# A two-layer hybrid decoder: the feed-forward layers in three parts of 6, 8 and 8 column pairs instead of four of 6, 6, 6 and 4, with a second Strassen double in the middle part, the gate's columns ahead of the up columns, and transfers queued behind those of the down projection

## The chip, the cores and the metric

One Trainium2 chip; the program runs on one of its cores. The time is the device time of one execution in microseconds, from the first to the last instruction and what lies around it; lower is better. PE is the matmul engine (PEld its weight loads), DVE the vector engine, ACT the activation engine, POOL the general engine, SP the engine that only issues transfers. [...] Each engine works through its own instructions in the order in which they were built, and waits where an operand isn't ready.

## The reference

The model has two layers on a stream of 512 tokens by 1024 features, all in float32. Layer 0 mixes with a state-space block, layer 1 with attention. Both end in the same feed-forward layer, which is all that the change touches:

```
def causal_dwconv(u, w, b):
    k_w = w.shape[0]
    s = u.shape[1]
    up = jnp.pad(u, ((0, 0), (k_w - 1, 0), (0, 0)))
    y = up[:, 0:s] * w[0]
    for k in range(1, k_w):
        y = y + up[:, k:k + s] * w[k]
    return y + b

def conv_ffn(x, ln_g, up_w, conv_w, conv_b, down_w):
    u = causal_dwconv(rms_norm(x, ln_g) @ up_w, conv_w, conv_b)
    gate, up = u[..., :FFN_DIM], u[..., FFN_DIM:]
    return (jax.nn.silu(gate) * up) @ down_w
```

`up_w` is 1024 x 5632 (2816 gate columns, then 2816 up columns), `conv_w` has three taps, `down_w` is 2816 x 1024. The result is added to the stream: `x = x + ff`.

## The kernel before, in words

**Precision and weights.** Every float32 matmul is made of three: each operand is split into a high half (an ACT copy to a rounded type) and a low half (a DVE subtraction), and high by high, high by low and low by high are added up in a PSUM bank (`mm3`, line 242). Weights stream from memory in chunks of 128 x 1024 into a ring of three raw tiles (`wr`), and are split into two rings of three tiles (`wh`, `wl`). The list `plan` holds all chunks in order; `chunk` (line 234) hands one to PE and has the split issued for two chunks ahead. When a chunk is issued, a function from `hooks` filed under its name is called: this is how a later step's loads are started.

**Pairs.** 128 gate columns and the 128 up columns of the same number make a pair; there are 22 (numbers 0 to 21). `whole` (line 1034) multiplies one pair by the normalised stream: two chunks of weights, each with half of the eight row blocks for both sides, 24 matmuls of 512 columns per chunk, gate and up taking turns. `taps` (line 1048) makes the convolution: one ACT instruction and two DVE instructions for each side; SiLU on ACT, the product on DVE (`gated`). `operands` (line 1291) then makes the seven token-side operands of a Strassen product for each two neighbouring pairs, a *double*: sums and high and low halves, in tiles `sh`, `sl`.

**Strassen doubles.** `double` (line 1149) computes two neighbouring pairs in another way: seven products (in the order 5, 1, 2, 6, 7, 3, 4) of 24 matmuls of 256 columns. Four of its weight combinations are made by transfers: a tile is loaded, and POOL's queue adds a second block to it (`up_plus`, line 1114), and a third once the first product's split has read it. `up_ahead` (line 1119) starts this: two loads on SP's queue, one accumulation on POOL's.

**Parts.** The 22 pairs are cut into parts (`PARTS_D`, line 32). When the pairs of a part are done, its down projection follows, again by seven Strassen products in the order of `SEVEN`: in layer 0 (`down_features`) of 256-column matmuls and features by tokens, in layer 1 (`down_tokens`) of 512 columns, added into `xr`. Weights come by loads (`down_load`) and accumulations (`plus`, line 1223): in layer 1 one tile `wz` serves products 1, 5, 6 and 4, each after one more accumulation. A part of four pairs in layer 1 has a form of its own (`short`), which adds with DVE instead.

**Order.** PE's order is written out: `KINDS` says for each part which doubles are plain (P) or Strassen (S); `STEPS` gives the steps of each part but the first, where P is a chunk of a plain pair, a digit a product of the Strassen double, and D the down projection of the part *before*. So each down projection starts two chunks (one pair) into the next part. The other engines' orders are made by the scheduler from the order of the program. Before, the second part of each layer had one Strassen double (pairs 8 and 9), and everything else was plain.

Of the kernel before, what the change touches and what calls it, by code (L numbers as in the profile page):

```python
# [18 lines left out]
P = 128  # L19
# [12 lines left out]
PARTS_D = (0, 6), (6, 12), (12, 18), (18, 22)  # L32
KINDS = "PPP", "PSP", "PPP", "PP"
STEPS = "PPPPPPPPPPPP", "PPDPPP51P26P734P", "PPDPPPPPPPPPP", "PPDPPPPPP"
# [10 lines left out]
def trunk_kernel(ctx: ExitStack, tc, x, ssm_ln_g, ssm_in_w, ssm_conv_w, ssm_conv_b, ssm_dt_bias,  # L45
# [84 lines left out]

# [898 lines left out]
    def ffn(l, norm, bp, gnext, nnext):  # L1029
        with (tc.tile_pool(name="ffn_h%d" % l, bufs=1) as hp, tc.tile_pool(name="ffn%d" % l, bufs=1) as fp,  # L1030
# [192 lines left out]
            def plus(t, p0, c, nq, j, i):  # L1223
                pool.dma_start(view(t, nq), source(p0, c, nq, j, i), accum_op=ALU.add)  # L1224

            def down_load(p0, n, k, c):
# [4 lines left out]
                sync.dma_start(view(raws[k][c], nq), source(p0, at, nq, j, i))  # L1231
                if k == "z" and not l:
                    plus(raws[k][c], p0, at, nq, 1, 1)
                if l and n == 4 and k != "y":
                    t, j = raws[k][1], k == "x"
                    sync.dma_start(view(t, nq), source(p0, at, nq, int(j), 0))
                    if not j:
                        plus(t, p0, at, nq, 0, 1)

            def short(m, p0, c, nq):  # L1240

                (z, z2), (x_, w), (y, _) = (raws[k] for k in "zxy")
                t = {"1": z, "2": w, "7": x_, "3": y}.get(m, z2)
                more = {"7": y, "6": y, "4": w}.get(m)
                if more is not None:
                    dve.tensor_tensor(out=t, in0=t, in1=more, op=ALU.add)
                return t

            def down_ahead(p0, n, ks):
                for k in ks:  # L1250
                    for c in range((n // 2 + 1) // 2 if l else 2):
                        down_load(p0, n, k, c)

            def combine(key, m, p0, c, nq):
# [5 lines left out]
                few = l and (p0, p0 + 4) in PARTS_D  # L1260
                if few:
                    t = short(m, p0, c, nq)
                elif m == "2" or (m == "4" and not l):
# [15 lines left out]
                if more and not few:  # L1279
# [269 lines left out]
            for i in range(1, len(parts)):  # L1549
# [7 lines left out]
                elif l:  # L1557
                    hooks[key] = lambda p0=p0, n=n: down_ahead(p0, n, "zxy")
# [483 lines left out]
```

## Time and profile before

| | us |
|---|---|
| three runs | 1350.83, 1354.39, 1353.06 (median 1353.06) |
| the profiled execution | 1350.98 |
| its span | 1349.3 |
| mean granted clock of the matmul engine | 0.991 of full speed |

The page's second part cuts the span into 40 equal slices of 33.7 us and gives the busy share of each in tenths:

```profile
PE   9999999999999999999997999999999989999997
PEld 8878888888887999988986778777888869788885
DVE  7899888788879867967759867678789857986877
PEclk9999999999999999999998999999999989999999
```

The feed-forward layer of layer 0 takes roughly slices 11 to 21, that of layer 1 slices 29 to 39; in between lies the attention. Times given as A:B are microseconds from the start of the span. In a list of waits a row names who waited at which line for whom, then the total, the number and the longest. A row of the chain has a start, a length, the engine, the tile and the line. The low halves of weights are `wl_h` (plain pairs), `wl_U` (Strassen doubles) and `wl_s` (down projection).

### The profile page before, as it was taken

How to read it: one execution, taken by the hardware profiler on the slowest of the kernel's cores; microseconds unless marked ns; L12 is line 12 of the kernel's file. 1: busy time of each engine (PE TensorE's matmuls, PEld its weight loads, DVE VectorE, ACT ScalarE, POOL GpSimd, SP SyncE). 2: the span in 40 equal slices, each digit the busy share in tenths (PEclk: the TensorE clock that was granted, in tenths of full speed). 3: DMA queues.
4: the chain of work that ended last, by engine and by line, in shares of the span. 5: the costliest groups of instructions: out<-in, count | busy, mean ns of one | idle time of the engine just before them, and what ended most of it. 6: DMA issues, size and time to landing. Idle time of an engine off the chain costs nothing.

```text
span 1349.3 us, 18914 instructions
## 1 busy us (share of the span) xinstructions
PE 1316.9 (98%) x6915; PEld 1106.9 (82%) x6915; DVE 1089.8 (81%) x1825; ACT 737.5 (55%) x1224; POOL 172.8 (13%) x205
## 2 busy tenths in 40 slices
PE   9999999999999999999997999999999989999997
PEld 8878888888887999988986778777888869788885
DVE  7899888788879867967759867678789857986877
ACT  6695554652567445544435657777566425544442
POOL 5320301200111310200203200000200110100100
PEclk9999999999999999999998999999999989999999
DMA  7543533431566893763743844221233664562631
GB/s 205 160 149 94 148 101 111 138 97 55 154 192 189 180 209 121 147 161 79 154 97 86 222 96 127 63 79 55 66 99 118 156 148 125 118 164 86 149 94 62
DMA packets 203005, 170.52 MB, mean 126 GB/s; under 512 B 9308, under 2 KB 176608, under 8 KB 202912
## 3 DMA queue, kind: packets, MB, share of 16 engines
q1 hardware_dynamic: 173728, 125.46, 31.1%
q0 software_dynamic: 25728, 38.56, 15.4%
q10 hardware_dynamic: 3456, 5.30, 1.2%
q8 instruction: 54, 0.88, 0.3%
q14 instruction: 39, 0.32, 0.1%
HBM read 162.84 MB, written 6.44 MB: 125 GB/s over the span
## 4 chain that ended last, share of the span: by engine, by line
PE 86%; DVE 7%; ACT 2%; DMA 2%; issue 1%; POOL 0%; DVEq 0%; SPq 0%; ACTq 0%; POOLq 0%
PE ps_in L243 5%; PE ps_in L245 5%; PE ps_in L244 5%; PE ps_g L245 5%; PE ps_g L243 5%; PE ps_g L244 5%; PE ps_u L243 5%; PE ps_u L244 5%; PE ps_u L245 5%; PE ps_s L1434 3%; PE ps_s L1429 3%; PE ps_s L1432 3%; PE ps_o L244 2%; PE ps_o L245 2%; PE ps_o L243 2%; PE ps_s L1333 2%
## 5 line engine op out<-in xcount | busy, mean ns | idle before, releaser
L245 PE MATMUL ps_g<-xgh,wl_h 128*128 128x512 f32 x320 | 124.6, 389 | 0.9 <-DVE wl_h L193 0.9
L243 PE MATMUL ps_g<-xgh,wh_h 128*128 128x512 f32 x320 | 124.9, 390 | 0.0
L244 PE MATMUL ps_g<-xgl,wh_h 128*128 128x512 f32 x320 | 124.6, 389 | 0.0
L243 PE MATMUL ps_u<-xgh,wh_h 128*128 128x512 f32 x320 | 124.6, 389 | 0.0
L244 PE MATMUL ps_u<-xgl,wh_h 128*128 128x512 f32 x320 | 124.5, 389 | 0.0
L245 PE MATMUL ps_u<-xgh,wl_h 128*128 128x512 f32 x320 | 124.5, 389 | 0.0
L243 PE MATMUL ps_in<-xgh,wh_in 128*128 128x512 f32 x304 | 122.9, 404 | 0.0
L245 PE MATMUL ps_in<-xgh,wl_in 128*128 128x512 f32 x304 | 119.7, 394 | 0.0
L244 PE MATMUL ps_in<-xgl,wh_in 128*128 128x512 f32 x304 | 119.2, 392 | 0.0
L182 ACT ACTIVATE wh_h<-wr_h 128x1024 fp32r<-128x1024 f32 x80 | 84.4, 1055 | 59.9 <-PE ps_u L244 33.9
L193 DVE TENSOR_TENSOR wl_h<-wr_h,wh_h 128x1024 fp32r<-128x1024 f32 x80 | 98.0, 1229 | 19.3 <-ACT wh_h L182 14.6
L1224 POOL DMA_DIRECT2D wz<-in_ffn_down_w_dram x43 | 51.3, 1258 | 468.7 <-DVE wl_s L1275 219.6
L1059 DVE SCALAR_TENSOR_TENSOR vg<-ps_g,cf,vg 128x511 f32<-128x511 f32 x72 | 53.8, 748 | 52.5 <-ACT vg L1057 51.9
L1074 ACT ACTIVATE sh<-vg 128x512 fp32r<-128x512 f32 (+1 forms) x88 | 48.9, 572 | 79.0 <-DVE vg L1146 52.7
L1432 PE MATMUL ps_s<-sh,wh_s 128*128 128x256 f32 x308 | 79.8, 286 | 6.7 <-ACT sh L1074 5.4
L1434 PE MATMUL ps_s<-sl,wh_s 128*128 128x256 f32 x308 | 79.8, 286 | 0.4 <-DVE sl L1075 0.2
L1274 ACT ACTIVATE wh_s<-wz 128x768 fp32r<-128x768 f32 (+2 forms) x52 | 43.4, 835 | 63.6 <-DMA wz<-in_ffn_down_w_dram 32.6
L1331 PE MATMUL ps_s<-wh_s,sh 128*128 128x512 f32 x153 | 61.9, 405 | 11.9 <-ACT wh_s L1274 6.5
L245 PEld LDWEIGHTS ps_g<-xgh,wl_h 128*128 128x128 f32 x320 | 60.1, 188 | 13.8 <-DVE wl_h L193 1.3
L245 PEld LDWEIGHTS ps_u<-xgh,wl_h 128*128 128x128 f32 x320 | 60.1, 188 | 12.6
L244 PEld LDWEIGHTS ps_u<-xgl,wh_h 128*128 128x128 f32 x320 | 60.1, 188 | 12.5
L243 PEld LDWEIGHTS ps_u<-xgh,wh_h 128*128 128x128 f32 x320 | 60.0, 188 | 12.5
(492 smaller groups left out, 3580.2 us busy)
## 6 DMA issues: line engine op xcount, KB each, us to landing
wr_h<-in_ffn_up_w_dram SPq DMA_DIRECT2D x160, 256.0 KB, 3.6
wr_in<-in_ssm_in_w_dram SPq DMA_DIRECT2D x40, 512.0 KB, 3.9
m<-cumd POOLq DMA_DIRECT2D x16, 512.0 KB, 4.3
wr_out<-in_ssm_out_w_dram SPq DMA_DIRECT2D x16, 512.0 KB, 3.5
wz<-in_ffn_down_w_dram POOLq DMA_DIRECT2D x18, 384.0 KB, 6.3
wz<-in_ffn_down_w_dram POOLq DMA_DIRECT2D x10, 512.0 KB, 5.8
wr_s<-in_ffn_down_w_dram SPq DMA_DIRECT2D x12, 384.0 KB, 3.4
xT<-in_ffn_down_w_dram SPq DMA_DIRECT2D x9, 512.0 KB, 5.5
```

The costliest lines, as they stand in the source:

```text
L182: return act.activation(self.wh[:, :self.n], self.raw[:, :self.n], AF.Copy)
L193: return eng.tensor_tensor(out=self.wl[:, :self.n], in0=self.raw[:, :self.n], in1=self.wh[:, :self.n].bitcast(F32), op=ALU.subtract)
L243: pe.matmul(ps, wh, xh, start=start, stop=False)
L244: pe.matmul(ps, wh, xl, start=False, stop=False)
L245: return pe.matmul(ps, wl, xh, start=False, stop=stop).ins
L1059: dve.scalar_tensor_tensor(out=v[:, s:], in0=u[:, :T - s], scalar=tap_col(j, p, 2 - s), in1=v[:, s:], op0=ALU.mult, op1=ALU.add)
L1074: act.activation(hi, v, AF.Copy)
L1224: pool.dma_start(view(t, nq), source(p0, c, nq, j, i), accum_op=ALU.add)
L1274: act.activation(wh[:, :n], t[:, :n], AF.Copy)
L1331: pe.matmul(pss[b], h, ws[q][0][:, cols], start=first and q == qs[0], stop=False, skip_group_check=more)
L1432: pe.matmul(v[:, b], wh[:, q, cols], h, start=opens and q + b == 0, stop=False, skip_group_check=not opens or b > 0)
L1434: pe.matmul(v[:, b], wh[:, q, cols], w, start=False, stop=False, skip_group_check=not opens or b > 0)
```

## The change

The parts become (0, 6), (6, 14), (14, 22); the middle part has the doubles plain, Strassen, plain, Strassen (pairs 8 and 12). From pair 2 on, a chunk of `whole` holds all eight row blocks of one side, so the gate's 24 matmuls come first and the up side's 24 after them. In layer 1 the loads and accumulations of the Strassen doubles, and the first loads of the last part's down projection, are issued on POOL's queue, behind the last accumulation of the down projection that runs then. The operands of an eight-pair part's fourth double stand in the tiles of the Strassen doubles' sums (`sE`), which are free by then. The four-pair form goes.

```diff
-PARTS_D = (0, 6), (6, 12), (12, 18), (18, 22)
-KINDS = "PPP", "PSP", "PPP", "PP"
-STEPS = "PPPPPPPPPPPP", "PPDPPP51P26P734P", "PPDPPPPPPPPPP", "PPDPPPPPP"
+PARTS_D = (0, 6), (6, 14), (14, 22)
+KINDS = "PPP", "PSPS", "PPPP"
+STEPS = "PPPPPPPPPPPP", "PPDPP51P26734P51P26P734", "PPDPPPPPPPPPPPPPP"
+WHOLE = 2
...
+                elif kind == "P" and p >= WHOLE:
+                    plan.append(("h%d_%d_%d" % (l, p, n), *w_cols(ffn_up_w[l], 0, KB, n * FFN + p * P, P)))
...
-                    wh, wl = (t.rearrange("p (k j) c -> p k j c", j=2) for t in chunk("h%d_%d_%d" % (l, p, c)))
+                    wh, wl = chunk("h%d_%d_%d" % (l, p, c))
+                    if p >= WHOLE:
+                        for k in range(KB):
+                            mm3(pss[c], wh[:, k], wl[:, k], xgh[k], xgl[k], k == 0, k == KB - 1)
+                        yield
+                        continue
+                    wh, wl = (t.rearrange("p (k j) c -> p k j c", j=2) for t in (wh, wl))
...
             def up_ahead(p):
                 z, x_ = ups[p] = spare.pop(0), spare.pop(0)
-                sync.dma_start(up_view(z), up_source(p, 0, 1))
-                up_plus(z, p, 1, 1)
-                sync.dma_start(up_view(x_), up_source(p, 0, 0))
+                eng = pool if l else sync
+                with tc.issue_after(state["plus"]) if l else nullcontext():
+                    eng.dma_start(up_view(z), up_source(p, 0, 1))
+                    if l:
+                        eng.dma_start(up_view(x_), up_source(p, 0, 0))
+                    up_plus(z, p, 1, 1)
+                if not l:
+                    sync.dma_start(up_view(x_), up_source(p, 0, 0))
...
-                pool.dma_start(view(t, nq), source(p0, c, nq, j, i), accum_op=ALU.add)
+                state["plus"] = pool.dma_start(view(t, nq), source(p0, c, nq, j, i), accum_op=ALU.add).ins
...
+            def down_behind(p0, n):
+
+                with tc.issue_after(state["plus"]):
+                    down_ahead(p0, n, "zxy", pool)
...
-                    sh = hp.tile([P, 7, 256], F32R, tag="sh", name="sh%d" % p, bufs=3)
-                    sl = hp.tile([P, 7, 256], F32R, tag="sl", name="sl%d" % p, bufs=3)
+                    if any(p == p1 - 2 and p1 - p0 == 8 for p0, p1 in PARTS_D):
+                        sh, sl = (flat(t)[:, :7 * 256].rearrange("p (s t) -> p s t", s=7) for t in sE)
+                    else:
+                        sh = hp.tile([P, 7, 256], F32R, tag="sh", name="sh%d" % p, bufs=3)
+                        sl = hp.tile([P, 7, 256], F32R, tag="sl", name="sl%d" % p, bufs=3)
...
-                    hooks[key] = lambda p0=p0, n=n: down_ahead(p0, n, "zxy")
+                    hooks[key] = lambda p0=p0, n=n: down_behind(p0, n)
```

What this moves on the engines, at three places. Rows are instructions in the engine's order: line, operation, output and inputs, size.

*POOL, layer 1, from the first down projection into the Strassen doubles.* `wz1_0` and `wz1_1` are the tile of products 1, 5, 6 and 4; `xT` from `in_ffn_up` is a tile of a Strassen double. Before:

```order
L1224 DMA wz1_0_9356<-in_ffn_down_w_dram 128x2x512
L1224 DMA wz1_1_9357<-in_ffn_down_w_dram 128x512
L1115 DMA xT_85<-in_ffn_up_w_dram 128x4x256
L1224 DMA wz1_0_9356<-in_ffn_down_w_dram 128x2x512
L1224 DMA wz1_1_9357<-in_ffn_down_w_dram 128x512
L1115 DMA xT_85<-in_ffn_up_w_dram 128x4x256 x2
```

And now:

```order
L1238 DMA wz1_0_9319<-in_ffn_down_w_dram 128x2x512
L1238 DMA wz1_1_9320<-in_ffn_down_w_dram 128x512
L1132 DMA xT_85<-in_ffn_up_w_dram 128x4x256
L1134 DMA xT_85<-in_ffn_up_w_dram 128x4x256
L1132 DMA xT_85<-in_ffn_up_w_dram 128x4x256
L1124 DMA xT_85<-in_ffn_up_w_dram 128x4x256
L1134 DMA xT_85<-in_ffn_up_w_dram 128x4x256
L1124 DMA xT_85<-in_ffn_up_w_dram 128x4x256 x5
```

Before, a double's accumulation (line 1115) stood ahead of the last two accumulations of the down projection, those for product 4. Now both of those (the first two rows) stand ahead, and the loads of both doubles (lines 1132 and 1134), formerly on SP, follow them.

*DVE, layer 0, behind product 3 of the Strassen double at pair 8.* In `wl_h0_11_0` the first number is the layer, then the pair and the chunk; `vg` and `vu` are the gate and up sides after the taps. Before:

```order
L1191 TENSOR_TENSOR u00_8_4805<-ps_U50_8_4813,u00_8_4805 128x2x256
L193 TENSOR_TENSOR wl_h0_12_0_5103<-wr_h0_12_0_5099,wh_h0_12_0_5102 128x1024
L1059 SCALAR_TENSOR_TENSOR vg0_8_5089<-u00_8_4805,cf0_90,vg0_8_5089 128x511
L1059 SCALAR_TENSOR_TENSOR vg0_9_5093<-u00_8_4805,cf0_90,vg0_9_5093 128x511
L1059 SCALAR_TENSOR_TENSOR vg0_8_5089<-u00_8_4805,cf0_90,vg0_8_5089 128x510
L1059 SCALAR_TENSOR_TENSOR vg0_9_5093<-u00_8_4805,cf0_90,vg0_9_5093 128x510
L193 TENSOR_TENSOR wl_h0_12_1_5163<-wr_h0_12_1_5159,wh_h0_12_1_5162 128x1024
```

And now, 19 rows behind the same instruction (line 1205 now):

```order
L1315 TENSOR_TENSOR vg0_8_4992<-vg0_9_4996,vg0_8_4992 128x256
L1068 SCALAR_TENSOR_TENSOR vu0_10_5093<-ps_u0_10_4834,cf0_90,vu0_10_5093 128x510
L1316 SCALAR_TENSOR_TENSOR vg0_9_4996<-vg0_9_4996,vg0_8_4992 128x256
L1084 TENSOR_TENSOR sl8_5039<-vg0_8_4992,sh8_5038 128x512
L1317 SCALAR_TENSOR_TENSOR vg0_9_4996<-vg0_9_4996 128x256
L1160 TENSOR_TENSOR vg0_10_5088<-vg0_10_5088,vu0_10_5093 128x512
L196 TENSOR_TENSOR wl_h0_11_0_5107<-wr_h0_11_0_5104,wh_h0_11_0_5106 128x1024
```

Before, the next plain chunks' low halves stood among the taps of the gate, a few rows behind product 3. Now the second double's products 5 and 1 stand there, and the low half of pair 11's gate comes behind all taps and most operand steps of the double.

*DVE, layer 0, last part, behind the last pair's matmuls.* `sl20` and `sEl0` are the low operands of the last double. Before:

```order
L1059 SCALAR_TENSOR_TENSOR vg0_21_6707<-ps_g0_21_6647,cf0_90,vg0_21_6707 128x511
L1275 TENSOR_TENSOR wl_s01_18_0_6729<-wx0_1_3672,wh_s01_18_0_6728 128x512
L1059 SCALAR_TENSOR_TENSOR vg0_21_6707<-ps_g0_21_6647,cf0_90,vg0_21_6707 128x510
L1059 SCALAR_TENSOR_TENSOR vu0_21_6712<-ps_u0_21_6648,cf0_90,vu0_21_6712 128x511
L1059 SCALAR_TENSOR_TENSOR vu0_21_6712<-ps_u0_21_6648,cf0_90,vu0_21_6712 128x510
L1146 TENSOR_TENSOR vg0_21_6707<-vg0_21_6707,vu0_21_6712 128x512
```

And now:

```order
L1068 SCALAR_TENSOR_TENSOR vg0_21_6502<-ps_g0_21_6442,cf0_90,vg0_21_6502 128x511
L1068 SCALAR_TENSOR_TENSOR vg0_21_6502<-ps_g0_21_6442,cf0_90,vg0_21_6502 128x510
L1277 TENSOR_TENSOR wl_s01_14_0_6524<-wz0_1_3670,wh_s01_14_0_6523 128x1024
L1068 SCALAR_TENSOR_TENSOR vu0_21_6507<-ps_u0_21_6443,cf0_90,vu0_21_6507 128x511
L1068 SCALAR_TENSOR_TENSOR vu0_21_6507<-ps_u0_21_6443,cf0_90,vu0_21_6507 128x510
L1160 TENSOR_TENSOR vg0_21_6502<-vg0_21_6502,vu0_21_6507 128x512
```

The rows are nearly the same; but the gate's taps read a bank that PE now finishes 24 matmuls before the up side's, where before both were finished three matmuls apart.

More of the change, by code (lines that the diff above doesn't have):

```diff
@@ L1223, in plus, with down_load @@
             def plus(t, p0, c, nq, j, i):
-                pool.dma_start(view(t, nq), source(p0, c, nq, j, i), accum_op=ALU.add)
-            def down_load(p0, n, k, c):
+                state["plus"] = pool.dma_start(view(t, nq), source(p0, c, nq, j, i), accum_op=ALU.add).ins
+            def down_load(p0, n, k, c, eng=sync):
                 j, i = ({"z": (0, 0), "x": (0, 1), "y": (1, 1)} if l else {"x": (0, 0), "z": (0, 1)})[k]
@@ L1230, in down_load, with down_ahead @@
                 at = 2 * c if l else c
-                sync.dma_start(view(raws[k][c], nq), source(p0, at, nq, j, i))
+                eng.dma_start(view(raws[k][c], nq), source(p0, at, nq, j, i))
                 if k == "z" and not l:
                     plus(raws[k][c], p0, at, nq, 1, 1)
[L1234 to L1249, printed above, removed]
+            def down_ahead(p0, n, ks, eng=sync):
                 for k in ks:
                     for c in range((n // 2 + 1) // 2 if l else 2):
-                        down_load(p0, n, k, c)
+                        down_load(p0, n, k, c, eng)
+            def down_behind(p0, n):
+                with tc.issue_after(state["plus"]):
+                    down_ahead(p0, n, "zxy", pool)
             def combine(key, m, p0, c, nq):
@@ L1259, in combine @@
                 n = nq * ncol
[L1260 to L1263, printed above, removed]
+                if m == "2" or (m == "4" and not l):
                     t = wrp.tile([P, 1024], F32, tag="raw", name="wr_" + key)
@@ L1278, in combine @@
                 more = ({"1": (0, 1), "5": (1, 1), "6": (1, 0)} if l else {"1": (0, 1), "5": (0, 0), "6": (1, 0)}).get(m)
-                if more and not few:
+                if more:
                     plus(t, p0, c, nq, *more)
```

## The prediction

> **What bounds the kernel now.** I read the page first, then the list of waits of the matmul engine, then the windows by stage, then the chain of waits around each gap.
>
> ```profile
> span 1349.3 us, 18914 instructions
> PE 1316.9 (98%) x6915; PEld 1106.9 (82%) x6915; DVE 1089.8 (81%) x1825; ACT 737.5 (55%) x1224; POOL 172.8 (13%) x205
> PE 86%; DVE 7%; ACT 2%; DMA 2%; issue 1%; POOL 0%; DVEq 0%; SPq 0%; ACTq 0%; POOLq 0%
> ```
>
> PE is busy nearly all the time and makes up 86% of the chain that ended last. So time is gained in two ways only: fewer matmul steps, or gaps closed. The gaps, from the list of waits (total us, times, longest):
>
> ```profile
> PE ps_s L1331 <- ACT wh_s L1274: 6.5, 2, 6.4
> PE ps_s L1432 <- ACT sh L1074: 5.4, 1, 5.4
> PE ps_s L1331 <- ACT sh L1074: 4.3, 2, 3.5
> PE ps_q L1642 <- DVE wl_q L208: 2.5, 2, 2.2
> PE ps_s L1432 <- DVE xT L1407: 1.3, 1, 1.3
> ```
>
> All of these lie in or right behind down projections (ps_s). Busy PE hides the pace, since matmuls overlap; the chain shows it, with start, length and count:
>
> ```profile
> 488.59 0.23 PE ps_u L243
> ...
> 502.46 0.48 PE ps_U L1176 x4
> ...
> 1061.79 0.91 PE ps_s L1328 x4
> ```
>
> A 512-column matmul costs 0.227 us (0.91/4), a 256-column one 0.120 (0.48/4). With that, the windows of five of the eight down parts (length; PE busy and count; weight loads; DVE; clock; DMA share; GB/s) give what each loses:
>
> ```profile
> 548.80:579.40 30.60, 30.45 (x252) 30.21 (x251) 8.93 (x13) 1.00 0.92 200
> 707.60:737.20 29.60, 22.63 (x168) 21.93 (x167) 8.19 (x12) 0.88 0.44 98
> 1059.80:1098.00 38.20, 31.64 (x126) 25.12 (x125) 10.07 (x16) 0.91 0.69 162
> 1161.70:1191.70 30.00, 28.82 (x126) 23.39 (x126) 10.07 (x16) 1.00 0.83 191
> 1318.40:1345.00 26.60, 20.99 (x81) 15.71 (x80) 10.96 (x18) 0.94 0.14 47
> ```
>
> Layer 0, second part: 30.6 - 252 x 0.120 = 0.4 lost. Layer 0, last part: 29.6 - 168 x 0.120 = 9.4. Layer 1, first: 38.2 - 126 x 0.227 = 9.6. Layer 1, second: 1.4. Layer 1, last: the code has 7 x 2 x 2 x 3 = 84 matmuls (81 recorded), so 26.6 - 19.1 = 7.5. Where the clock is below 1.00, part of the loss is not the wait but the slow matmuls behind it.
>
> **Matmul work.** In each layer one plain double of pairs becomes a Strassen double. A plain one is 2 x 48 matmuls of 512 columns, 96 x 0.227 = 21.8 us; a Strassen one is 7 x 24 of 256 columns, 168 x 0.120 = 20.2. Two layers: **-3.3 us**. The down parts keep their count (11 doubles per layer). What the fourth part's adds and the six extra adds of the four-pair form took on DVE goes too, but only where DVE was waited for does that count, below.
>
> **Layer 1, first down part (9.6).** The chain through its gap:
>
> ```profile
> 1070.62 7.46 DMA xT<-in_ffn_up_w_dram
> ...
> 1078.65 0.50 POOL xT L1115
> ...
> 1079.39 10.70 DMA wz<-in_ffn_down_w_dram
> 1090.20 1.06 ACT wh_s L1274
> 1091.30 0.79 PE ps_s L1331
> ```
>
> ```profile
> 1076.46 1.83 DVE L1275 TENSOR_TENSOR wl_s<-wz,wh_s 128x1024 fp32r<-128x1024 f32 x2 [3.14 <-ACT wh_s L1274]
> ```
>
> The accumulating transfers for product 4 could start once DVE had read the two tiles (about 1077.6 and 1078.3). They start at 1079.4, behind the pair's accumulation that waits for its own load to land on POOL's queue, and then take 10.7 us beside the two up loads. PE idles from 1084.9 to 1091.3 (the 6.4 of the list) and then runs slow for a while: the stage's clock is 0.91, and 9.6 less 6.4 is 3.2 more. The new order has the two accumulations first and the up loads behind them on the same queue. The next rows give the usual landing:
>
> ```profile
> wz<-in_ffn_down_w_dram POOLq DMA_DIRECT2D x10, 512.0 KB, 5.8
> xT<-in_ffn_up_w_dram POOLq DMA_DIRECT2D x3, 512.0 KB, 5.9
> ```
>
> 1077.6 + 5.8 = 1083.4, plus the copy of 1.06 = 1084.5, just when PE needs it. Bounds: nothing regained (10.7 again) to all 9.6. I take 1.0 left: **-8.6**. Price of the move: the loads for the Strassen pair start later, about 1079 to 1083 behind POOL's issues, land by 1086, their accumulation by 1093 (two times 5.9); the first Strassen product, with the gap gone, comes at 1088 + one plain pair of 10.9 = 1099. SP loses four transfers of the pairs and six of the last part; the next on it are the up weights of pairs 7 and 10, which can only gain. Behind the new waits on POOL stand the pairs' accumulations and nothing else; its ten new transfers are 13 us of issuing on an engine that is 13% busy.
>
> **Layer 0, last down part (9.4) and the query projection.** Behind the last matmul of pair 21:
>
> ```profile
> 708.32 0.77 ACT L1057 ACTIVATE vu<-ps_u,cf 128x512 f32<-128x512 f32 x1
> ...
> 709.87 1.52 DVE L1059 SCALAR_TENSOR_TENSOR vu<-ps_u,cf,vu 128x511 f32<-128x511 f32 x2
> 711.50 0.69 DVE L1146 TENSOR_TENSOR vg<-vg,vu 128x512 f32<-128x512 f32 x1
> ...
> 713.42 0.58 PE L1432 MATMUL ps_s<-sh,wh_s 128*128 128x256 f32 x1 [5.42 <-ACT sh L1074]
> ```
>
> With the gate's 24 matmuls first, its taps, SiLU and a weight copy are done 5.4 us earlier. The up side then starts at 707.9 instead of 708.3 on ACT and at 708.7 instead of 709.9 on DVE: 1.1 us sooner. The first product now runs over four doubles, so six matmuls (0.7) instead of two (0.2) come before the late one. Stall 5.4 becomes about 4.0; with the low half (0.5) and a half-pace stretch of 1.2, 5.7 stays. The 1.3 behind DVE L1407 goes: a chunk is 24 matmuls (2.9 us) where it was 12 (1.4), against one split and two half-tile steps on DVE. **-3.7**. By the same slack the query weights, split 2.2 us late, come in time: PE then has both chunks of product 3 (5.8 us instead of 2.9) while DVE splits. With the half-pace matmuls behind it (nine at 0.43 as below, where 0.23 is normal: 1.9) the place lost about 4.4; I take **-4.2**, with bounds 0 and -4.5.
>
> ```profile
> 744.30 0.43 PE ps_q L1641
> ```
>
> **Layer 1, last down part (7.5).** It waits 3.5 us for pair 21's operands in product 2, since product 1 over two doubles covers only 12 matmuls, 2.7 us. Over four doubles product 1 covers 5.4, and the late double's place in product 2 comes another 3.2 later. The wait in product 5 (0.75 and 0.4) moves out alike, but there DVE has only some 0.4 us to spare by the count of its order. I leave 0.8: **-6.7**.
>
> **What the second Strassen double costs.** DVE must bring each product's weights and a long tail of taps and operands. Spacing on DVE, start to start:
>
> ```profile
> 531.49 2.73 DVE L1059 SCALAR_TENSOR_TENSOR vg<-u,cf,vg 128x511 f32<-128x511 f32 x4
> 534.14 1.22 DVE L193 TENSOR_TENSOR wl_h<-wr_h,wh_h 128x1024 fp32r<-128x1024 f32 x1
> 535.27 2.80 DVE L1059 SCALAR_TENSOR_TENSOR vu<-u,cf,vu 128x511 f32<-128x511 f32 x4
> ...
> 540.85 0.68 DVE L1075 TENSOR_TENSOR sl<-vg,sh 128x512 fp32r<-128x512 f32 x1
> 541.45 0.42 DVE L1309 TENSOR_TENSOR vg<-vg 128x256 f32<-128x256 f32 x1
> 541.78 0.74 DVE L1059 SCALAR_TENSOR_TENSOR vu<-ps_u,cf,vu 128x511 f32<-128x511 f32 x1
> ```
>
> A tap takes 0.66, a split 1.13, a 512-wide step 0.60, a 256-wide one 0.33. *Layer 0, pair 11:* from the end of product 3 of the double at pair 8 to the low half of pair 11's gate stand 3 splits, 12 taps, 6 steps of 512 and 5 of 256: 3.4 + 7.9 + 3.6 + 1.7 = 16.6. PE has product 4 (2.9), a chunk (5.4), two products (5.8) and two matmuls (0.4) until it needs that half: 14.5. New stall 2.1. *Layer 0, down behind the part:* after product 3 of the double at pair 12 come 3 splits, 9 taps, 7 and 6 steps: 3.4 + 5.9 + 4.2 + 2.0 = 15.5, started 0.5 late; PE has 2.9 + 10.9 + 0.7 = 14.5. Stall 1.5 instead of 0.4. Together **+3.2**; bounds 0 and, with a half-pace stretch behind each, +6. *Layer 1:* the same tail is needed later there (product 1 wants only the first operand), but before product 4 DVE has to add two down tiles, and waits for the second's load, which comes after the double has read its tile:
>
> ```profile
> 1137.27 1.23 DVE L1269 TENSOR_TENSOR xT<-xT 128x1024 f32<-128x1024 f32 x1 [2.40 <-DMA xT<-in_ffn_down_w_dram]
> ```
>
> That wait now falls on the double nearest to the down part, so I count 1.5 lost there instead of 1.4: **+0.1**. Elsewhere the splits have room: before, the parts between downs have no gap.
>
> **Sum:** -3.3 - 8.6 - 3.7 - 4.2 - 6.7 + 3.2 + 0.1 = **-23.2**. The profiled execution took 1350.98 (span 1349.3), so 1327.8. The median of the three runs is 1353.06, 2.1 above it; as the runs go, **1330**.
>
> **Rivals.**
>
> (1) The up loads on POOL come late. [...]
>
> ```profile
> L1224 POOL DMA_DIRECT2D wz<-in_ffn_down_w_dram x43 | 51.3, 1258 | 468.7 <-DVE wl_s L1275 219.6 <-DMA xT<-in_ffn_down_w_dram 70.2 <-DVE vg L1305 48.1
> ...
> L749 POOL DMA_DIRECT2D er<-cumd x24 | 12.6, 530 | 75.6 <-DVE xs L845 73.7 <-DMA cumd<-cumT 1.8
> ```
>
> 1.26 us each in the FFN against 0.53 elsewhere. If load and accumulation take the 10.7 seen above each, the chain is 1079 + 1.3 + 10.7 + 1.3 + 10.7 + 2.3 for copy and split = 1105, 6 after PE's 1099, and 2 of half pace: 1338. Against it: 10.7 was seen with SP's loads beside it. [...]
>
> (2) The change does not close the 9.6: the accumulation is late by its own chain of four through one tile, and the up loads still share the wires. Then 8.6 comes back: 1338.
>
> (3) DVE's tails are worse than counted, in both layers: two more stalls of 2 us and a half-pace stretch of 2 at each: 1338.
>
> (4) Slower: DVE becomes the bound of the two middle parts. Counted so, DVE has 68 us (layer 0) and 74 (layer 1) in 84 of PE. With POOL at work, splits can stretch:
>
> ```profile
> 727.40 1.80 DVE L1275 TENSOR_TENSOR wl_s<-wx,wh_s 128x512 fp32r<-128x512 f32 x1
> ```
>
> 1.80 where a 512-wide step above took 0.68. If each of some 25 splits per part lost 1.1, 27 us, DVE would need 95 to 101, 11 to 17 over PE: 28 in all, past the gain of 23 from 11.6 per layer on: 1358. Against it: one such row, in a stretch where POOL computes sums; the split quoted above, in a stage with POOL's transfers, keeps its 1.22.
>
> **How the numbers follow.** Chances: forecast 0.62 (1324 to 1335), rivals (1) 0.09, (2) 0.11, (3) 0.10, all three together, about 1349 to 1354, 0.04; (4) 0.04. 0.3% is 4 us, about what a measurement of this kernel can tell from no change. Faster: 0.62 + 0.30 = 0.92, same 0.04, slower 0.04. The range goes from the forecast without any of the small remainders (1.0, 0.8, 0.3 and 3.3 less: 1325) to rivals (1) to (3), with the 2 us to 3 us by which the runs shown scatter: 1322 to 1340.
>
> **What would show it.** First down part of layer 1 near 29.6 us at clock 1.00; last of layer 0 near 46 (336 x 0.12 + 5.7); last of layer 1 near 39; a wait of ps_g on DVE wl_h of some 2 us before pair 11 in layer 0; no wait of ps_q on wl_q; U matmuls x672 at 0.120. Wrong if ps_U waits for xT or wh_U, or if DVE waits stand between the products.

## The result and the profile after

The changed kernel takes **1331.66 us** (median of four runs, 1330.09 to 1334.15); the kernel before, beside it, 1352.15 (1350.83 to 1354.39). The ratio is 0.9845, with a 95% interval of 0.9824 to 0.9865. The forecast was 1330, 1.7 below. The times in bold are medians; one execution of a later kernel (upsp) took 4636.12 us, more than three times its others, and is left out of its median.

The profiled executions stand a little worse: the one of after is the slowest of its four (1334.15, span 1332.5), the one of before near its fastest (1350.98, span 1349.3). Step by step this pair has a gain of 16.8 us to share out, not 20.5, and the prediction's own sum was 23.2.

The list of waits of the matmul engine, after (who waited at which line for whom, us in total, times, longest):

```profile
PE ps_s L1437 <- ACT sEh L1083: 6.2, 2, 4.8
PE ps_g L247 <- DVE xgl L1084: 3.6, 3, 2.0
PE ps_g L248 <- DVE wl_h L196: 2.3, 1, 2.3
PE ps_g L246 <- ACT xgh L1083: 0.8, 2, 0.5
PE ps_s L1439 <- DVE sEl L1084: 0.6, 2, 0.4
```

The longest wait of before, ps_s for a weight copy (6.5), is gone, and so is ps_q for wl_q. What waits now is ps_s for operands, and a newcomer that the prediction had nowhere: ps_g for x itself (xgl and xgh), in a stage that had not been looked at.

The six down parts of after, by windows, of the instructions on ps_s alone (length; PE busy and count; weight loads; DVE; then for the core the granted clock, the DMA share and GB/s):

```profile
461.00:491.30 30.30, 29.95 (x250) 30.14 (x251) 8.92 (x13) 1.00 0.96 206
579.40:623.50 44.10, 41.97 (x334) 41.76 (x335) 8.95 (x13) 0.96 0.82 178
699.70:747.60 47.90, 42.52 (x335) 42.21 (x336) 8.94 (x13) 0.93 0.52 109
1062.20:1090.80 28.60, 28.27 (x125) 23.62 (x126) 10.08 (x16) 1.00 0.70 162
1174.70:1213.80 39.10, 38.22 (x167) 31.31 (x168) 10.07 (x16) 1.00 0.81 191
1289.90:1327.60 37.70, 37.31 (x165) 30.97 (x165) 10.86 (x17) 1.00 0.54 112
```

Layer 1's three parts run at full clock, and the second alone still loses 1.0 us; layer 0's second and third show a clock of 0.96 and 0.93, since slow matmuls follow a stall there.

For every stage the table gives what it loses: from its first matmul to that of the next stage, less its matmuls by their pace (0.227 us for 512 columns, 0.120 for 256, full counts). "up" is the stage of gate and up columns ahead of a down part.

| stage | before | after | change | predicted |
|---|---|---|---|---|
| matmul work, two Strassen doubles more | | | -3.3 | -3.3 |
| layer 0, first up | 2.0 | 7.6 | **+5.6** | 0 |
| layer 0, middle up and its down part | 0.4 | 4.3 + 3.8 | **+7.7** | +3.2 |
| layer 0, last down | 9.4 | 7.4 | -2.0 | -3.7 |
| first part of the query projection (26.9 us, then 22.3) | | | -4.6 | -4.2 |
| from there to layer 1's feed-forward (214.2, then 209.3) | | | **-4.9** | 0 |
| layer 1, first up | 5.2 | 7.0 | +1.8 | 0 |
| layer 1, first down | 9.6 | 0.0 | -9.6 | -8.6 |
| layer 1, second down (with 0.2 of the third that goes) | 1.6 | 1.0 | -0.6 | +0.1 |
| layer 1, last down | 7.5 | 0.0 | -7.5 | -6.7 |

The rows add up to -17.4; the span shrank by 16.8, since 1.0 is lost ahead of the first feed-forward layer and 0.3 gained behind the last down part. The first row of layer 0 is the least steady: where that stage is the same as in before it loses 2.0 (before), 3.2 (b_pool) and 3.1 us (b_w3), and where it is the same as in after 7.6 (after) and 6.5 to 6.7 (upsp, l0one and dahead, the kernels of the next section).

### The profile page after: what moved, and what is told of

The parts are those of the page before. It is cut to its first block, busy times and chain, and to the rows that moved or that the text cites. A ratio compares the mean times of both kernels' runs of the same rounds, so it can differ in the third digit from the quotient of the medians.

```text
span 1332.5 us, 18904 instructions
## 1 busy us (share of the span) xinstructions
PE 1312.7 (99%) x7059; PEld 1112.0 (83%) x7059; DVE 1072.4 (80%) x1785; ACT 745.8 (56%) x1223; POOL 185.2 (14%) x212
## 3 DMA queue, kind: packets, MB, share of 16 engines
q1 hardware_dynamic: 164272, 119.68, 30.2%
## 4 chain that ended last, share of the span: by engine, by line
PE 91%; DVE 5%; ACT 2%; DMA 1%; issue 1%; DVEq 0%; ACTq 0%; SPq 0%
PE ps_in L246 5%; PE ps_in L248 5%; PE ps_in L247 5%; PE ps_g L247 4%; PE ps_g L248 4%; PE ps_g L246 4%; PE ps_u L246 4%; PE ps_u L247 4%; PE ps_u L248 4%; PE ps_s L1434 3%; PE ps_s L1439 3%; PE ps_s L1437 3%; PE ps_s L1333 2%; PE ps_s L1336 2%; PE ps_s L1338 2%; PE ps_o L247 2%
## 5 line engine op out<-in xcount | busy, mean ns | idle before, releaser
L248 PE MATMUL ps_u<-xgh,wl_h 128*128 128x512 f32 x288 | 112.3, 390 | 0.0
L1238 POOL DMA_DIRECT2D wz<-in_ffn_down_w_dram x28 | 33.8, 1216 | 305.3 <-DVE wl_s L1277 202.4
L247 PEld LDWEIGHTS ps_g<-xgl,wh_h 128*128 128x128 f32 x288 | 54.9, 191 | 15.8 <-DVE xgl L1084 4.9
L1276 ACT ACTIVATE wh_s<-wz 128x1024 fp32r<-128x1024 f32 (+2 forms) x38 | 37.3, 981 | 54.2 <-DMA wz<-in_ffn_down_w_dram 15.0
L248 PEld LDWEIGHTS ps_in<-xgh,wl_in 128*128 128x128 f32 x304 | 57.1, 188 | 12.1 <-issue 0.4
L246 PEld LDWEIGHTS ps_in<-xgh,wh_in 128*128 128x128 f32 x304 | 57.2, 188 | 11.8 <-issue 1.3
L247 PEld LDWEIGHTS ps_in<-xgl,wh_in 128*128 128x128 f32 x304 | 57.2, 188 | 11.0 <-issue 0.5
L246 PEld LDWEIGHTS ps_g<-xgh,wh_h 128*128 128x128 f32 x288 | 54.8, 190 | 12.7 <-ACT xgh L1083 1.7
L1439 PE MATMUL ps_s<-sl,wh_s 128*128 128x256 f32 x252 | 65.2, 287 | 0.0
L1437 PE MATMUL ps_s<-sh,wh_s 128*128 128x256 f32 x252 | 65.1, 286 | 0.0
```

The source lines that it names most:

```text
L246: pe.matmul(ps, wh, xh, start=start, stop=False)
L247: pe.matmul(ps, wh, xl, start=False, stop=False)
L248: return pe.matmul(ps, wl, xh, start=False, stop=stop).ins
L1238: state["plus"] = pool.dma_start(view(t, nq), source(p0, c, nq, j, i), accum_op=ALU.add).ins
L1276: act.activation(wh[:, :n], t[:, :n], AF.Copy)
L1437: pe.matmul(v[:, b], wh[:, q, cols], h, start=opens and q + b == 0, stop=False, skip_group_check=not opens or b > 0)
```

## The experiments

All kernels ran beside the kernel before, on the same chip in each group. After itself ran in the first group only, and the medians of the kernel before go from 1351.45 to 1352.87 over the groups, so differences from after are known to about 1 us. "Lost" is the measure of the table above.

### Whole columns from pair 3 (w3)

```diff
-WHOLE = 2
+WHOLE = 3
```

> The kernel after, with pair 2's chunks by halves of the row blocks as before the change (whole columns from pair 3 on). Theory A: the first parts lost 5.6 us in layer 0 (72.2 us from pair 0's third chunk to the down part, before 66.6) and 1.8 in layer 1 (67.2, before 65.4) because pair 2's gate alone now needs all eight row blocks of x within 5.4 us, 2.7 us earlier for the last four than with chunks by halves. Then both windows return (66.6 and 65.4), the waits of ps_g for xgl and xgh go, and the time is 1331.7 - 7.4 = 1324. Rival B: the late operands come from ACT, which waited 3.8 us for the key weights' load in front of the copies of x; then a wait of some 2 us stays in layer 0 and the time is 1328 or more.

**1327.28 us** (1326.72 to 1328.19), ratio 0.9811 [0.9793, 0.9829]. What it answers to, first in after's timeline of DVE and ACT (start, us, engine, line, operation; in brackets the idle time ahead of it and what ended it) where pair 2's gate runs:

```profile
401.22 1.34 ACT L1011 ACTIVATE stage<-stage,c 128x512 f32<-128x512 f32 x2 [3.78 <-DMA stage<-in_kv_w_dram]
402.46 1.04 ACT L1083 ACTIVATE xgh<-wx 128x1024 fp32r<-128x1024 f32 x1
...
403.60 1.22 DVE L1084 TENSOR_TENSOR xgl<-wx,xgh 128x1024 fp32r<-128x1024 f32 x1
405.95 0.69 DVE L1160 TENSOR_TENSOR vg<-vg,vu 128x512 f32<-128x512 f32 x1 [1.14 <-ACT vg L1473]
406.56 1.22 DVE L1084 TENSOR_TENSOR xgl<-wx,xgh 128x1024 fp32r<-128x1024 f32 x1
```

The last four row blocks of x come at 404.8 and 407.8. With a chunk of half the row blocks for both sides PE gets to them after 24 matmuls, 5.4 us into the pair; with the gate alone after 12, 2.7 us in. In w3 the same wait is

```profile
PE ps_g L247 <- DVE xgl L1084: 0.4, 1, 0.4
```

and the first up stages lose 3.0 and 5.1 instead of 7.6 and 7.0: 6.4 us between the profiled executions, 4.4 between the medians. Theory A holds for the cause, though the time is 3 us above its 1324: layer 0's stage lasts 67.6 us by its window and not 66.6, and after's profiled execution, from which the 7.4 came, is its slowest. ACT's 3.8 us behind a load of key weights (rival B) is there in w3 too (3.7), but alone it leaves no more than 0.4 of waiting with the old chunks for pair 2.

### No whole columns (wnone)

```diff
-WHOLE = 2
+WHOLE = NPAIR
```

> The kernel after, with no whole columns at all (each chunk four row blocks of both sides, as before the change). Theory A, from the prediction: the last down part of layer 0 gets back the 1.1 us that the earlier gate had saved (lost 7.4 now, then 8.5 and more), the query projection keeps its gain, since that comes from the two chunks of product 3 of the longer part; the first parts get their 7.4 back: 1331.7 - 7.4 + 1.1 = 1325. Rival B: the query projection's gain of 4.7 hangs on the whole columns too: then ps_q waits for wl_q again and the time is 1330.

**1337.34 us** (1335.96 to 1339.17): slower than after, so both theories missed, by 7 us and more. The first up stages gained as in w3, and the query projection kept its whole gain (22.3 us, no wait for wl_q), which theory A had said. But four stages became worse than in w3: layer 0's last down part (9.2 for 7.3), layer 1's middle up stage (2.1 for 0.0), its last down part (1.2 more), and above all its second down part, 7.1 lost for 0.8. One became better: layer 0's middle up stage, with pair 11 in it, loses 2.1 for 4.3. In that second down part PE waits for a split, by wnone's list of waits:

```profile
PE ps_s L1333 <- DVE wl_s L1277: 4.2, 1, 4.2
```

and DVE, with that split, stands behind ACT, by wnone's timeline of ACT:

```profile
1172.93 2.00 ACT L1276 ACTIVATE wh_s<-wr_s 128x1024 fp32r<-128x1024 f32 x2
1179.14 1.06 ACT L1276 ACTIVATE wh_s<-wz 128x1024 fp32r<-128x1024 f32 x1 [4.21 <-DMA wz<-in_ffn_down_w_dram]
1180.10 0.61 ACT L1083 ACTIVATE sEh<-vg 128x512 fp32r<-128x512 f32 x1
```

ACT works in order: a weight copy that waits 4.2 us for its transfer stands ahead of the last double's operand (sEh). With whole columns that operand's two copies come at 1173.4 and 1176.4 by w3's timeline, ahead of and between the copies that wait (1.4 and 1.0 us there). So whole columns from pair 3 on are worth some 10 us with the long parts (1337.3 less 1327.3), where the prediction counted 1.1 for the gate's earlier taps.

### Layer 1's loads for the Strassen doubles back on SP (upsp)

```diff
-                eng = pool if l else sync
-                with tc.issue_after(state["plus"]) if l else nullcontext():
-                    eng.dma_start(up_view(z), up_source(p, 0, 1))
...
+                sync.dma_start(up_view(z), up_source(p, 0, 1))
+                up_plus(z, p, 1, 1)
+                sync.dma_start(up_view(x_), up_source(p, 0, 0))
```

> The kernel after, with layer 1's loads of the Strassen doubles issued on SP at once, as before the change, instead of on POOL behind the last accumulation of the down part. Theory A, from the prediction: the first down part of layer 1 waits again 6 us for product 4's wh_s and lasts 38 instead of 28.6 us: 1340. Rival B: the gap was closed by the new parts and chunks, not by the order of the queues: the window stays below 30 and the time at 1332. Rival C: only part of it comes back, since the accumulation waits for its own load alone: 1335.

**1339.14 us** (1337.41 to 1339.72, three runs): theory A, which had 1340, though the window is 36.4 us and not 38. The chain through the gap in upsp (start, length, engine, tile, line):

```profile
1071.01 6.01 DMA xT<-in_ffn_up_w_dram
...
1077.58 0.73 POOL xT L1124
...
1078.33 11.07 DMA wz<-in_ffn_down_w_dram
...
1089.51 1.07 ACT wh_s L1271
```

The accumulation for product 4 stands behind the pair's accumulation, which waits 6.0 us for its own load, and then takes 11.1 itself; PE waits 5.6. In after POOL has (timeline):

```profile
1078.04 1.20 POOL L1238 DMA_DIRECT2D wz<-in_ffn_down_w_dram  x1 [6.44 <-DVE wl_s L1277]
1079.46 0.90 POOL L1238 DMA_DIRECT2D wz<-in_ffn_down_w_dram  x1 [0.22 <-issue]
1080.23 0.93 POOL L1132 DMA_DIRECT2D xT<-in_ffn_up_w_dram  x1
```

The first copy of what they bring runs at 1083.9, 5.8 us after the issue began, as estimated from the usual landing. The down part loses 0.0 in after and 7.8 in upsp. By the DVE timelines the tile had been read at 1075.5 in upsp, 2.9 us ahead of the transfer's start at 1078.3, and at 1077.7 in after, 0.3 ahead of its issue. So 2.6 us are the place behind the pair's accumulation and 5.3 the longer transfer (11.1 for 5.8), together what the part loses. Whether that transfer is longer because the pair's accumulation is ahead of it on the queue, or because the pair's loads share the moment, no run takes apart.

### The same edit on the kernel before (b_pool)

```diff
-                sync.dma_start(up_view(z), up_source(p, 0, 1))
-                up_plus(z, p, 1, 1)
-                sync.dma_start(up_view(x_), up_source(p, 0, 0))
+                eng = pool if l else sync
+                with tc.issue_after(state["plus"]) if l else nullcontext():
...
```

> The kernel before with one edit: layer 1's loads of the Strassen double are issued on POOL behind the last accumulation of the down part that runs, in the new order. Theory A, from the prediction: the gap of the first down part of layer 1 goes without the new parts (window 38.2 to some 29.5 us): 1352.9 - 8.6 = 1344. Rival B: half of the gap stays, since the accumulations wait for their own load and share the wires with the two loads: 1348. Rival C: nothing comes, the new parts are what closed it: 1352.

**1344.71 us** (1343.23 to 1345.16), ratio 0.9948 [0.9931, 0.9965], where the kernel before of that group took 1351.45. Window of the first down part of layer 1 in b_pool:

```profile
1061.00:1091.20 30.20, 29.10 (x126) 23.42 (x126) 10.06 (x16) 1.00 0.63 150
```

38.2 has become 30.2, 8.0 less. Theory A again: the move behind the accumulations on POOL's queue closes this gap but for 1.5 us, without the new parts. From both sides, then, this edit is worth 6.7 (here) to 7.5 us (upsp), by the medians.

### The last part's first loads back on SP (dahead)

```diff
-                    hooks[key] = lambda p0=p0, n=n: down_behind(p0, n)
+                    hooks[key] = lambda p0=p0, n=n: down_ahead(p0, n, "zxy")
```

> The kernel after, with the first loads of the last down part of layer 1 on SP at once, as before the change, instead of on POOL behind the last accumulation. Theory A, from the prediction, which gave this edit no term of its own: the loads have two plain doubles' time and more, nothing waits for them, 1331.7 with or without (within 2). Rival B: on SP they stand ahead of the up weights and wait for their tiles, so that a plain pair's weights come late by 4 us or more behind the second down part: 1336. Rival C: on SP they land early beside the accumulations of product 4 of the second down part, which comes late as in the first part before: window 1174.7:1213.8 grows from 39 to 43 us or more, 1336.

**1332.23 us** (1330.67 to 1333.93): as after. The second and last down parts lose 0.6 and 0.0. This half of the queueing is worth nothing that can be measured.

### One Strassen double in layer 0 (l0one)

```diff
-KINDS = "PPP", "PSPS", "PPPP"
+KINDS = ("PPP", "PSPP", "PPPP"), ("PPP", "PSPS", "PPPP")
...
+STEPS = (("PPPPPPPPPPPP", "PPDPPP51P26P734PPPPP", "PPDPPPPPPPPPPPPPP"),
```

> The kernel after, with one Strassen double instead of two in the middle part of layer 0 (plain, Strassen, plain, plain); layer 1 keeps two. Theory A: the second Strassen double costs layer 0 more than it saves: its tails on DVE make PE lose 4.2 us before pair 11's gate and 3.8 us at the down part behind; without it some 0.4 is lost there as in the kernel before, and 1.6 us of matmuls come back: 1331.7 - 7.6 + 1.6 = 1325.7. Rival B: the two stalls come from the eight-pair part and its DMA traffic, not from the second Strassen double; then half or more of the 8 stays, and the time is 1329 to 1333.

**1325.61 us** (1324.76 to 1326.78), ratio 0.9800 [0.9784, 0.9815]; theory A had 1325.7. Layer 0's middle up stage and its down part lose nothing:

```profile
575.40:615.70 40.30, 40.18 (x335) 40.26 (x336) 8.92 (x13) 1.00 0.80 182
```

So the second Strassen double, with the order of steps that was written for it, costs layer 0 8.0 us and saves 1.6 there. The edit changes both: the first double's steps are 51P26P734 behind three chunks, as in before, where after has 51P26734 behind two, with no chunk ahead of 734. Which of the two makes pair 11's weights late, no run takes apart. In layer 1, where nothing is lost in that stage (0.0 in after), the second double should pay by this table, but no run leaves it out there. Its price in layer 0 shows in after's timeline of PE at pair 11's gate, where the low half of the weights comes late:

```profile
539.55 0.40 PE L247 MATMUL ps_g<-xgl,wh_h 128*128 128x512 f32 x1
542.28 0.50 PE L248 MATMUL ps_g<-xgh,wl_h 128*128 128x512 f32 x1 [2.33 <-DVE wl_h L196]
542.62 0.40 PE L246 MATMUL ps_g<-xgh,wh_h 128*128 128x512 f32 x1
542.85 0.42 PE L247 MATMUL ps_g<-xgl,wh_h 128*128 128x512 f32 x1
543.08 0.62 PE L248 MATMUL ps_g<-xgh,wl_h 128*128 128x512 f32 x1
543.50 0.63 PE L246 MATMUL ps_g<-xgh,wh_h 128*128 128x512 f32 x1
543.93 0.63 PE L247 MATMUL ps_g<-xgl,wh_h 128*128 128x512 f32 x1
```

The starts stand 2.73 us apart at the gap instead of 0.23, and from 0.8 us behind it 0.43 apart: 2.5 of gap and 1.8 of slow matmuls make up the 4.3.

### Both gains together (l0one_w3)

The edits of l0one and w3 in one kernel.

> The kernel after with both edits that gained: one Strassen double in layer 0 (two in layer 1), and whole columns from pair 3 on. Theory A: they lie in different stages and add: 1331.7 - 6.1 - 4.4 = 1321. Rival B: they share a delay (the time that a stage starts late is caught up later), so that the two give less than 8 together: 1324 or more.

**1321.87 us** (1320.82 to 1322.54), ratio 0.9781 [0.9766, 0.9795]. They add; theory A, which had 1321.

### Product 1 first in layer 0's down projection (best_one, best_s1)

To the edits of l0one_w3 comes

```diff
-SEVEN = "5126743", "1257634"
+SEVEN = "1526743", "1257634"
```

> The kernel of the run before this (one Strassen double in layer 0, whole columns from pair 3), with layer 0's down projection beginning with product 1 instead of product 5. Theory A: the last down part of layer 0 loses 7.1 us because product 5 reads the sums of the late pair 21's operands, while product 1 reads those of pair 20 alone; 48 matmuls of 0.120 us then cover 5.8 of it, and 1 stays: 1321 - 6 = 1315. Rival B: product 1's weights come too late in front (their load was planned as the second), or product 5's operands are still late by 2 and the matmuls behind run slow: 1318 to 1321.

**1316.55 us** (1315.79 to 1317.10), ratio 0.9741 [0.9727, 0.9756]. The last down part of layer 0, by windows:

```profile
688.30:730.70 42.40, 40.77 (x336) 40.38 (x336) 8.91 (x13) 1.00 0.60 123
```

47.3 us (l0one_w3) have become 42.4, at a clock of 1.00; the wait for the late operand is 1.1 instead of 4.8. Theory A, with 2.1 left where it had 1, and 1316.55 for 1315. The same kernel in another group:

> The fastest kernel so far a second time, to see what two chip jobs of one kernel differ by: 1316.6 again, within 1.5.

**1317.47 us** (1315.81 to 1318.47), ratio 0.9747 [0.9731, 0.9763]: two groups differ by 0.9 us.

### The same with two Strassen doubles in layer 0 (w3_one), and with product 2 second (best_one_b)

> The kernel after with whole columns from pair 3 and product 1 first in layer 0's down projection, and two Strassen doubles in both layers. Theory A: product 1 covers the late operands of the second Strassen double too (3.8 us at the down part behind it), the 4.3 before pair 11's gate stay: 1327.3 - 3.8 - 6 = 1317.5, some 2.5 above the kernel with one double in layer 0. Rival B: the whole cost of the second double moves into another wait: 1320 to 1322.

This kernel is w3 with product 1 first. **1320.07 us** (1318.79 to 1320.63), 2.6 over theory A and inside rival B's range; but what B had as its reason did not come, since the cost moved to no other wait. Product 1 covers the late operands of the second Strassen double as well (0.4 lost at the down part behind it instead of 3.8); the 4.3 at pair 11's gate stay. The last down part gained 3.8 (7.3 to 3.6) and not the 6 that theory A had taken over from best_one's forecast, where 4.9 came: its two gaps are the same as in best_one (1.25 and 0.75 us), but here slow matmuls followed, there none (granted clock 0.50 and 1.00, the last section has the rows). That and the 0.4 are the 2.6. Then the same change of order in best_one:

```diff
-SEVEN = "1526743", "1257634"
+SEVEN = "1256743", "1257634"
```

> The fastest kernel so far (one Strassen double in layer 0, whole columns from pair 3, product 1 first) with product 2 as the second of layer 0's down projection and product 5 as the third. Theory A: the 2.1 us that the last down part still loses (1.1 and 0.5 of waits for pair 21's sums at product 5, and slow matmuls behind) go, since product 2 reads the plain operand of pair 21, which is written before the sums: 1316.6 - 1.5 = 1315, at the edge of what can be told apart. Rival B: product 2's weights, loaded straight from memory in front of product 5's, or the plain operand itself come late by as much: 1316 to 1318.

**1318.40 us** (1317.75 to 1319.38): no better than best_one, at the upper edge of rival B. Product 5's wait went, and ps_s waits 2.1 us for a split (wl_s) further on in its place; the first down part of layer 0 loses 1.4.

### Whole columns alone on the kernel before (b_w3)

The lines of the change for whole columns, from pair 3 on, in the kernel before: four parts, loads on SP.

> The kernel before with whole columns from pair 3 as its only edit (four parts, loads on SP). Theory A, from the prediction: the last down part of layer 0 loses 1.1 us less (9.4 to 8.3), and the 1.3 behind its first product go; the query projection still waits for wl_q, since product 3 of a four-pair part is as short as before: 1352 - 2 = 1350. Rival B: the earlier gate also lets the query weights come in time, either edit is enough: 1352 - 7 = 1345. Rival C: as in the run without whole columns, they matter in layer 1 too (its last part loses 7.5): 1348 or less by that window.

**1352.79 us** beside 1351.90, ratio 1.0004 [0.9995, 1.0014]: nothing, less than any theory had. The longest wait in layer 0's last down part did shrink by 1.0, as in theory A; the 1.3 behind the first product, which theory A had going too, stayed. List of waits of b_w3, where before had 5.4:

```profile
PE ps_s L1441 <- ACT sh L1083: 5.2, 2, 4.4
```

But the stage loses 9.5 us, as before (9.4): the matmuls behind the shorter gap lost 1.0 us more by running slow (2.7 over their pace, in before 1.7). The query's wait is still there (2.2), as theory A had it. Elsewhere small losses (layer 0's second down part 1.7 for 0.4, layer 1's last 9.9 for 7.5) and a gain (its first 8.2 for 9.6) cancel.

## Why the prediction was right, and where it was wrong

**Right in mechanism and size.** The loads behind the accumulations on POOL's queue (-8.6 forecast, -9.6 measured; upsp and b_pool show the cause from both sides, and b_pool leaves 1.5). The longer last part of layer 1 (-6.7, -7.5). The query projection (-4.2, -4.6), and that the two chunks of product 3 in a longer part bring it, not the whole columns: wnone keeps it, b_w3 doesn't get it. The Strassen doubles' pace is as counted (672 matmuls, 0.120 us). Of the rivals, (2) did not come (the window loses 0.0), (3) came in layer 0 alone (below), and (4) is refuted by layer 1's middle stage, which loses 0.0. Of the signs, the waits came as named and no wait of ps_U stands in the list; layer 0's last part took 47.9 us where 46 was named. The remark that three of the 84 matmuls of layer 1's last part went unrecorded misreads before's trace, which has six of 256 columns into the tile `end` in their place; the 7.5 is the same either way.

**Rival (1) did not happen, but by little.** The up loads on POOL landed later than I estimated: the first copy of one (wh_U) ran at 1096.1, its operand estimated for 1093. Both splits were done at 1099.6, PE came to them at 1102.0. b_pool's -6.7 shows that here the move gained.

**The step that was missing: pair 2 in the first parts** (+5.6 and +1.8). The prediction said "before, the parts between downs have no gap" and looked for what the gate's 24 matmuls bring at the end of a part, not for what they ask at its beginning: the last four row blocks of x from 2.7 us into the pair on, where the old chunks gave 5.4. In the kernel before their low halves were written at 403.8 and 405.6 by DVE's timeline, and PE read those of the fifth and the sixth block from 404.9 and 406.2 on: just in time. w3 shows it: 4.4 us of the time hang on a limit that is off by one pair. Of the +5.6, w3 gets back 4.6; the other 1.0 lies in the scatter of that stage (2.0 to 3.2 without the step), in which ACT's wait for the key weights differs too (2.4 us in before, 3.7 in w3).

**Mis-sized: "what the second Strassen double costs"** (+3.2, measured +7.7). The waits were nearly right: 2.3 at pair 11's gate where I had 2.1, 1.8 at the down part where I had 1.5 instead of 0.4. What I left at the upper bound and not in the value was the slow matmuls behind a stall, 1.6 to 1.8 at each; with them the cost passes even that bound, +6. I had seen such matmuls in three of the five windows of before.

**Mis-sized: "Layer 0, last down part"** (-3.7, measured -2.0). I let the up side start 1.1 us sooner on DVE, at 708.7 where before's last matmul of the pair starts at 707.4, so 1.3 behind it, and left a stall of 4.0. In after's chain:

```profile
700.00 1.07 ACT wh_s L1276
701.09 1.23 DVE wl_s L1277
702.32 0.67 DVE vu L1068
703.01 0.76 DVE vu L1068
```

A weight copy and its split are released by one of PE's last matmuls and come ahead of the up side's taps. By the timelines these begin 2.4 us behind the start of the last matmul (702.23 and 699.80), in before 2.5 (709.87 and 707.38), so they come only 0.1 sooner. In b_w3, with the gate first too, they begin 1.5 behind it: in a four-pair part such a copy and split are 512 wide and in b_w3's chain take 0.64 and 0.69; for eight pairs they are twice as wide, 1.07 and 1.23, which is the 1.0 that I had not counted. So the stall is 4.8 and not 4.0, and the slow matmuls behind it take 1.7 and not 1.2. The whole columns are worth much at another place instead: 10 us between wnone and w3, most of it in layer 1's second down part, of which the prediction said nothing.

**Not predicted: 4.9 us behind the query projection.** 3.3 of them are one gap ahead of the transposes of the keys (ktq), present in before, b_pool and b_w3, absent in all kernels whose query projection doesn't wait. That it follows from that wait is likely, since before's chain leads from the late split of the query weights (740.3) to these transposes (778.3); but the three kernels with the gap are also the three with four parts, and no run here takes the two apart.

Taken together: the missing step and the two mis-sized ones are 13.6 us short of the forecast (5.6, 1.8, 4.5, 1.7), the gains that were larger than said give 7.8 back (1.0, 0.8, 0.7, 0.4 and the 4.9), and -23.2 becomes the table's -17.4. That the median is within 1.7 of 1330 is in part luck. The errors one way and the other cancel for more than half, with 4.9 from a stage of which the prediction said nothing. The profiled execution came out 6.4 above the 1327.8 forecast for it; of this, 2.2 are what the forecast of the median had added, and 2.5 are what after's profiled execution stands above its own median.

A kernel that beats both came out of it: best_one, 1316.55 us, 15 below after and 35 below before. It keeps the parts and the queue, has one Strassen double in layer 0's middle part, whole columns from pair 3, and product 1 first.

## What to carry to other kernels

When a block of work is put in another order, ask for both ends: what its last operand releases sooner, and what its first half now needs sooner. Edits of an order are worth what they are worth together: whole columns alone gave nothing, with longer parts 10 us. On an engine that works in order (in wnone a weight copy that waited 4.2 us on ACT stood ahead of the last double's operand), a move that ends one wait lets the next queued instruction go first, so list what stands in front of the instruction that you want early. And when you price a stall, allow for the slow matmuls behind it: in after 1.6 to 1.8 us behind each of layer 0's three stalls from pair 11's gate on, in best_one none behind its waits of 1.1 and 0.5 us.

## What the runs showed of the hardware that was not expected

**The granted clock halved behind some stalls and not behind others of about the same length.** In after it is 0.50 from 406.5, 543.1, 584.0 and 703.5 us on, for 6.8, 3.4, 3.4 and 6.8 us. There a 512-column matmul takes 0.43 us instead of 0.227; the slow ones behind pair 11's stall cost 1.8. Windows of all instructions around three stalls (length; PE; weight loads; DVE; ACT; POOL; granted clock; DMA share; GB/s): pair 11's gate in after, the last down part of layer 0 in w3_one, and the same in best_one.

```profile
539.66:543.07 3.41, 1.08 (x5) 0.68 (x4) 3.41 (x6) 1.80 (x4) 0.00 (x0) 1.00 0.00 0
543.07:546.48 3.41, 3.41 (x9) 2.64 (x8) 3.41 (x5) 0.00 (x0) 0.00 (x0) 0.50 0.51 154
...
697.64:701.06 3.42, 1.84 (x14) 1.64 (x14) 3.42 (x8) 1.26 (x2) 1.04 (x1) 1.00 0.90 137
701.06:704.47 3.41, 3.41 (x18) 3.41 (x18) 2.39 (x3) 1.06 (x1) 0.00 (x0) 0.50 0.95 213
...
695.04:698.45 3.41, 1.89 (x13) 1.69 (x14) 3.41 (x7) 1.26 (x2) 0.95 (x1) 1.00 0.87 136
698.45:701.87 3.42, 3.42 (x31) 3.42 (x30) 2.40 (x3) 1.20 (x2) 0.00 (x0) 1.00 0.95 220
```

PE waited for the late operands 1.1 and 0.5 us in w3_one and in best_one, and was busy for 1.84 and 1.89 us of the first window; the half clock followed in w3_one alone. What decides that is not shown. So the length of a stall alone does not settle its price. The stage with pair 11 lost 4.3 us in after, with a wait of 2.3, and 2.1 in wnone, where no wait for wl_h is longer than 1.8. A wait of 2.2 was followed by half clock in before (ps_q; 0.53 from 742.0 to 745.3), one of 2.1 in best_one_b was not (256-column matmuls start 0.12 apart behind it). In before 4.4 us at half clock follow the restart in layer 0's last down part (713.4 to 717.8), and its chain has two 256-column matmuls at 0.43 us up to the row at 717.37; in b_w3's chain, behind the shorter gap, they still take 0.43 at 719.79 and 0.36 at 721.07, which is the 1.0 that ate its gain.

**One accumulating transfer took nearly twice as long in upsp as in after.** The accumulation for product 4 took 11.07 us in upsp, behind the pair's accumulation and beside its load; in after, ahead of them, 5.8 from the issue to the first copy.
